# Seven block products in place of eight for the three closing projections of a hybrid encoder step

## The chip, the core and the metric

The kernel runs on one core of one Trainium2 chip. Its time is the device time in microseconds (us) of one execution; several executions are timed and their median is the result. The engines of the core work side by side and are ordered only by semaphores: PE (the matrix engine, with PEld for its weight loads), DVE (vector), ACT (scalar), POOL (GpSimd) and SP, which here does nothing but issue the transfers, in the order of its queue. The profile is one execution taken by the hardware profiler.

## The reference, cut to what matters

One layer of a streaming encoder for 2048 prompt rows and 64 sample rows of width 1024, all in float32. The change lies in the last function alone; `att` and `pb` are the outputs of the two token mixers, `ga`, `gb` and `mg` columns of the input projection.

```python
h = rmsnorm(x, norm_g)
q, k, v, ga, u, gb, mg = split_proj(h, w_in)
att = stick_breaking(q, k_all, v_all)
pb = multi_scale_pool(u, buf, w_pool, pool_scale)

def merge_out(x, att, ga, pb, gb, mg, w_br_a, w_br_b, w_out):
    y_a = (att * jax.nn.silu(ga)) @ w_br_a
    y_b = (pb * jax.nn.silu(gb)) @ w_br_b
    gate = jax.nn.sigmoid(mg)
    m = gate[..., :D_MODEL] * y_a + gate[..., D_MODEL:] * y_b
    return x + m @ w_out

y = rmsnorm(merge_out(...), final_g)
```

The three products with `w_br_a`, `w_br_b` and `w_out` are each 2112 rows by 1024 by 1024.

## The kernel before

A float32 product is made of three matmuls of split operands. `split` (lines 79 and 80) writes `hi`, the operand rounded by a cast on ACT, and `lo`, what is left, by a subtraction on DVE; a product is `hi*hi + hi*lo + lo*hi`, the third small term left out.

The program is in three stretches. The first, up to line 880, makes projections, attention and pooling, a half of the rows at a time. It leaves in DRAM, transposed (channels by rows), the gated attention `aT_d`, the gated pooling `bT_d` and the merge gates `sm_d`. The second (lines 881 to 914) is the last fifteen slabs of the input projection (`proj`, lines 282 to 284), 128 columns each. Beside them `load_weight` brings `w_br_a` into SBUF, split into tiles of 128 rows by 512 columns, and `load_rows` the first block of rows. The raw parts come through a ring of two buffers, `wraw`.

The third stretch is the closing phases, from line 916. It opens tile pools of its own: `back` in SBUF and `bpsum` in PSUM, in the place that the pools of the first stretch gave up. `branch` runs twice, with `aT_d` and `w_br_a`, then with `bT_d` and `w_br_b`. For each block of 424 rows (`POST`) and each 128 output columns it adds 24 matmuls in one PSUM bank (lines 952 to 954: weights stationary, rows moving), multiplies the bank by the gate `sg` on DVE (line 956), adds in the second run the first run's result `mpl` (line 958), and stores the tile `bo` (line 959). The first run's output is `mp_d`, the second's `m_d`. The weights of the next run are loaded and split while this one works.

The output projection (lines 967 to 1027) takes row tiles of 128. There the split rows are stationary and the split `w_out` moves, 512 columns a matmul: two banks of 24 matmuls a tile (lines 1014 to 1016). The residual `xo` is added on DVE (line 1017), ACT sums the squares (line 1019), `rsqrt_of_mean` (lines 82 to 91) makes the scale on DVE and ACT, and line 1025 scales and line 1027 stores. The 64 sample rows take 32 matmuls (lines 1003 and 1006).

PE works in the order written in the program. The order of the other engines and of SP is made by the framework when it compiles: an instruction may be set earlier than it is written if its buffers and inputs are free then, but on the chip each queue is strictly in that fixed order. The framework also sets all semaphores, from the tiles that instructions read and write and from the buffers (`bufs=`) of each pool.

## Time and profile before

| | us |
|---|---|
| median of 3 executions (2823.55 to 2825.31) | 2824.5 |
| span of the profiled execution, first to last instruction | 2823.3 |
| last fifteen slabs of the input projection | 2092 to 2260 |
| both branch projections, first to last matmul start | 2260.4 to 2628.9 |
| output projection, first to last matmul start | 2629.5 to 2815.4 |
| from there to the end | 7.9 |

A row of a group in the profile names line, engine and operation, the tiles (output<-inputs), the shape (partitions x columns), the count, and after the bar the busy time in us and the mean of one in ns. Spans of matmuls overlap, since they are pipelined, so what one matmul costs is read from the distance of two starts, not from its span. In the view of transfers the last number of a row is the median time from issue to landing.

### The profile page before, as it was taken

To read this page: it belongs to the slowest core of one execution; us is meant where nothing else is said; L and a number is where in the kernel's file an instruction comes from. 1 tells how busy PE (TensorE), PEld (TensorE's weight loads), DVE (VectorE), ACT (ScalarE), POOL (GpSimd) and SP (SyncE) were. 2 spreads that over 40 slices of the span, in tenths; PEclk is the share of its full clock that TensorE was granted. 3 is DMA by queue.
4 is the path that set the end of the run, shared out by engine and by line. 5 is a ranking of instruction groups with operands and counts; after the bars stand their busy time and mean duration, and the time that the engine had idled before them with its cause. 6 is when DMAs were issued, how large, how long until landed. Compare 5 with 4: busy or idle time off the path is not lost.

```text
span 2823.3 us, 42058 instructions
## 1 busy us (share of the span) xinstructions
PE 2771.4 (98%) x15044; PEld 2415.1 (86%) x15044; DVE 1678.2 (59%) x2847; ACT 1194.2 (42%) x2500; POOL 447.9 (16%) x1107
## 2 busy tenths in 40 slices
PE   6999999999999999999999999999999999999998
PEld 5988898889998988888888888887778899999877
DVE  6555555577768683578887888885442022434543
ACT  4445444455555553455555555553223111211221
POOL 2112222220000002233343334330000000000000
PEclk9999999999999999999999999999999999999999
DMA  4223222234444454211111111113344264666432
GB/s 148 73 87 125 71 71 71 84 106 157 151 149 149 155 164 127 72 46 49 57 53 46 49 57 53 34 57 98 116 127 148 75 210 142 214 193 199 162 130 88
DMA packets 333309, 307.83 MB, mean 109 GB/s; under 512 B 30302, under 2 KB 288078, under 8 KB 333100
## 3 DMA queue, kind: packets, MB, share of 16 engines
q1 hardware_dynamic: 333100, 305.15, 34.4%
q8 instruction: 118, 1.93, 0.3%
q14 instruction: 91, 0.75, 0.1%
HBM read 208.99 MB, written 96.07 MB: 108 GB/s over the span
## 4 chain that ended last, share of the span: by engine, by line
PE 93%; DVE 4%; ACT 1%; DMA 1%; issue 1%; POOL 0%; SPq 0%; DVEq 0%; ACTq 0%; POOLq 0%
PE pj L282 17%; PE pj L284 17%; PE pj L283 17%; PE ps L952 4%; PE ps L953 4%; PE ps L954 4%; PE tr L636 4%; PE att L653 2%; PE att L652 2%; PE att L651 2%; PE ps L1015 2%; PE z L625 2%; PE ps L1016 2%; PE ps L1014 2%; PE z L624 2%; PE z L623 2%
## 5 line engine op out<-in xcount | busy, mean ns | idle before, releaser
L282 PE MATMUL pj<-hhi,whi 128*128 128x512 f32 (+2 forms) x2608 | 945.2, 362 | 0.0
L284 PE MATMUL pj<-hhi,wlo 128*128 128x512 f32 (+2 forms) x2608 | 917.9, 352 | 0.5 <-DVE wlo L80 0.5
L283 PE MATMUL pj<-hlo,whi 128*128 128x512 f32 (+2 forms) x2608 | 916.8, 352 | 0.1
L284 PEld LDWEIGHTS pj<-hhi,wlo 128*128 128x128 f32 x2608 | 491.9, 189 | 65.9 <-DVE wlo L80 1.0
L282 PEld LDWEIGHTS pj<-hhi,whi 128*128 128x128 f32 x2608 | 494.4, 190 | 59.6 <-ACT sgm L300 0.4
L283 PEld LDWEIGHTS pj<-hlo,whi 128*128 128x128 f32 x2608 | 493.4, 189 | 58.8 <-DVE hlo L80 0.4
L577 DVE TENSOR_TENSOR_SCAN om<-om 128x513 f32<-128x513 f32 (+3 forms) x356 | 388.0, 1090 | 212.5 <-POOL om L559 108.2
L567 ACT ACTIVATE om<-z 128x512 f32<-128x512 f32 (+2 forms) x320 | 171.3, 535 | 323.0 <-PE z L625 273.9
L80 DVE TENSOR_TENSOR wlo<-raw,whi 128x512 fp32r<-128x512 f32 x248 | 171.6, 696 | 199.8 <-ACT whi L79 198.8
L580 DVE TENSOR_TENSOR be<-be,om 128x512 f32<-128x512 f32 (+3 forms) x356 | 230.4, 647 | 31.4
L79 ACT CAST whi<-raw 128x512 fp32r<-128x512 f32 x256 | 158.1, 623 | 171.4 <-PE pj L283 154.0
L79 ACT CAST a<-tr 128x512 fp32r<-128x512 f32 (+2 forms) x356 | 188.1, 528 | 100.4 <-PE tr L636 89.7
L80 DVE TENSOR_TENSOR a<-tr,a 128x512 fp32r<-128x512 f32 (+2 forms) x356 | 215.8, 607 | 23.8 <-ACT a L79 21.7
L952 PE MATMUL ps<-rhi,bwhi 128*128 128x424 f32 (+1 forms) x640 | 226.7, 354 | 0.8 <-issue 0.8
L953 PE MATMUL ps<-rlo,bwhi 128*128 128x424 f32 (+1 forms) x640 | 226.8, 354 | 0.0
L954 PE MATMUL ps<-rhi,bwlo 128*128 128x424 f32 (+1 forms) x640 | 226.3, 354 | 0.0
L579 POOL COPY carry<-om 128x1 f32<-128x1 f32 x356 | 77.9, 219 | 921.7 <-DVE om L577 881.2
L79 ACT CAST rhi<-rraw 128x424 fp32r<-128x424 f32 (+4 forms) x128 | 66.3, 523 | 293.2 <-PE ps L954 221.6
L956 DVE TENSOR_TENSOR bo<-ps,sg 128x424 f32<-128x424 f32 (+1 forms) x80 | 47.8, 597 | 228.7 <-PE ps L954 216.3
L636 PE MATMUL tr<-ident,be 128*128 128x128 f32 x1088 | 176.0, 274 | 6.1 <-DVE be L580 3.6
L636 PEld LDWEIGHTS tr<-ident,be 128*128 128x128 f32 x1088 | 136.5, 140 | 44.9 <-DVE be L580 8.1
L568 ACT ACTIVATE be<-z 128x512 f32<-128x512 f32 (+2 forms) x320 | 170.1, 532 | 0.0
(180 smaller groups left out, 4111.3 us busy)
## 6 DMA issues: line engine op xcount, KB each, us to landing
raw<-in_w_in_dram SPq DMA_DIRECT2D x256, 256.0 KB, 3.1
kraw<-in_cache_k_dram SPq DMA_DIRECT2D x64, 256.0 KB, 3.5
vraw<-in_cache_v_dram SPq DMA_DIRECT2D x64, 256.0 KB, 2.9
sg<-sm_d SPq DMA_DIRECT2D x64, 212.0 KB, 2.6
sm_d<-sgm SPq DMA_DIRECT2D x48, 256.0 KB, 2.1
out_dram<-nat SPq DMA_DIRECT2D x42, 256.0 KB, 2.3
aT_d<-ao SPq DMA_DIRECT2D x32, 256.0 KB, 2.0
xo<-in_x_prompt_dram SPq DMA_DIRECT2D x16, 512.0 KB, 3.6
```

Of the source, the lines that this page charges most:

```text
L79: nc.scalar.copy(hi, src)
L80: (nc.gpsimd if eng == "g" else nc.vector).tensor_tensor(lo, src, hi.bitcast(F32), op=ALU.subtract)
L282: nc.tensor.matmul(ps[:, 0:n], whi[:, k], hhi[:, k, c0:c0 + n], start=k == 0, stop=False)
L283: nc.tensor.matmul(ps[:, 0:n], whi[:, k], hlo[:, k, c0:c0 + n], start=False, stop=False)
L284: nc.tensor.matmul(ps[:, 0:n], wlo[:, k], hhi[:, k, c0:c0 + n], start=False, stop=k == KT - 1)
L567: nc.scalar.activation(om[:, off:512], z[:, off:512], AF.Sigmoid, scale=-SCALE)
L577: nc.vector.tensor_tensor_scan(rev, rev, rev, 1.0, op0=ALU.mult, op1=ALU.bypass)
L580: nc.vector.tensor_tensor(be[:, off:512], be[:, off:512], om[:, off + 1:513], op=ALU.mult)
L636: nc.tensor.transpose(tr[:, i * P:(i + 1) * P], be[:, off + j * P:off + (j + 1) * P], ident)
L952: nc.tensor.matmul(ps[:, 0:n], whi[:, ws], hi[:, 0:n], start=k == 0, stop=False)
L953: nc.tensor.matmul(ps[:, 0:n], whi[:, ws], lo[:, 0:n], start=False, stop=False)
L954: nc.tensor.matmul(ps[:, 0:n], wlo[:, ws], hi[:, 0:n], start=False, stop=k == KT - 1)
```

## The change

Each 1024 by 1024 weight is cut into four blocks of 512 by 512, and the rows into pairs of blocks, so that a projection is a two by two product of blocks. Eight block products are replaced by seven, with sums of blocks as operands: the weight in seven forms (`WFORMS`: three plain blocks, four sums `t1` to `t4`) and the rows in seven forms (`r11`, `r12`, `s2`, `s1`, `r21`, `r12`, `r22`, of which the later `r21` and `r12` hold sums). Accumulators `x` and `y` in PSUM are read out in the midst of their accumulation (`kept`, `okept`), since a part of the sum serves several outputs.

`weight_sums` makes the sums of a weight on POOL and stores them in DRAM (`tw_d`). `load_form` loads and splits one form into a buffer of its own, so that all seven forms of a weight lie in SBUF; the buffer of a form is refilled for the next weight after its last use (`t == 2`). All raw parts of weights pass the ring of two buffers `wraw`, now 512 KB each. In the two branch projections 2112 rows are three pairs of 352 (`NR`). For each branch `i`, pair `t` and form `p` a pass of 48 matmuls runs, `make(s + 2)` preparing the row form two passes on, in two buffers; passes 1, 4, 5 and 6 end outputs (`emit`). The output projection takes pairs of 128-row tiles, 84 matmuls of 512 columns a pair; the sample rows keep plain products, of 40 matmuls, from the forms that are there. The rest of `out_sample`, `residual` and `finish` hold the same steps as before.

```diff
@@ constants and DRAM @@
-NB = 424
-POST = ((0, 424), (424, 424), (848, 424), (1272, 424), (1696, 416))
+NR = 352
+WFORMS = ("b11", "b21", "t2", "t1", "t3", "b22", "t4")
+    tw_d = dram.tile([3, 4, D // 2, D // 2], F32, name="tw_d")
@@ beside the last fifteen slabs of the input projection @@
-        wside = ctx.enter_context(tc.tile_pool(name="wside", bufs=1, side="right"))
-        def load_weight(w, out):
...
-        def load_rows(src, r0, n, into, out):
...
+        wright = ctx.enter_context(tc.tile_pool(name="wright", bufs=1, side="right"))
+        rowx = ExitStack()
+        rform = rowx.enter_context(tc.tile_pool(name="rform", bufs=1, side="right"))
+        wpool = {nm: wright for nm in WFORMS[:4]}
+        weights = (w_br_a[0], w_br_b[0], w_out[0])
+        def weight_sums(i):
+            for k in range(4):
+                top, bot = (wright.tile([P, 2, 512], F32, name="wraw", bufs=2) for _ in range(2))
+                for h, t in enumerate((top, bot)):
+                    r = h * 512 + k * P
+                    nc.sync.dma_start(t, weights[i][r:r + P, :].rearrange("p (j c) -> p j c", j=2))
+                b11, b12, b21, b22 = top[:, 0], top[:, 1], bot[:, 0], bot[:, 1]
+                for j, out, x, y in ((0, b11, b12, b11), (2, b12, b22, b12), (1, b22, b22, b11), (3, b21, b21, b22)):
+                    nc.gpsimd.tensor_tensor(out, x, y, op=ALU.subtract)
+                    nc.sync.dma_start(tw_d[i, j, k * P:(k + 1) * P, :], out)
+        def load_form(i, nm):
+            if nm[0] == "t":
+                src = tw_d[i, int(nm[1]) - 1]
+            else:
+                r, c = (int(x) - 1 for x in nm[1:])
+                src = weights[i][r * 512:(r + 1) * 512, c * 512:(c + 1) * 512]
+            sv = src.rearrange("(k p) c -> p k c", p=P)
+            hi = wpool[nm].tile([P, 4, 512], F32R, name=f"{nm}hi")
+            lo = wpool[nm].tile([P, 4, 512], F32R, name=f"{nm}lo")
+            for k in (0, 2):
+                raw = wright.tile([P, 2, 512], F32, name="wraw", bufs=2)
+                nc.sync.dma_start(raw, sv[:, k:k + 2])
+                split(hi[:, k:k + 2], lo[:, k:k + 2], raw)
+            return hi, lo
+        def row_form():
+            return (rform.tile([P, 4, NR], F32R, name="rhi", bufs=2),
+                    rform.tile([P, 4, NR], F32R, name="rlo", bufs=2))
+        wf, rf = {}, {}
+        def before_closing():
+            yield from weight_sums(0)
+            for nm in WFORMS[:4]:
+                wf[0, nm] = load_form(0, nm)
+                yield 1.0
+            for p in range(2):
+                hi, lo = rf[p] = row_form()
+                for k in (0, 2):
+                    raw = wright.tile([P, 2, 512], F32, name="wraw", bufs=2)
+                    src = aT_d[p * 512 + k * P:p * 512 + (k + 2) * P, 0:NR].rearrange("(k p) r -> p k r", p=P)
+                    nc.sync.dma_start(raw[:, :, 0:NR], src)
+                    split(hi[:, k:k + 2], lo[:, k:k + 2], raw[:, :, 0:NR])
+                yield 1.0
+        run((chain(*[proj(GROUPS_B, [merge_gate(1, c)]) for c in range(1, 2 * KT)]), 15 * slab_ns(1)),
+            (before_closing(), 11.0))
@@ the two branch projections @@
-        def branch(w, src, gate0, dst, add, rows0=None):
...
-        branch(wa, aT_d, 0, mp_d, None, rows0)
-        rows0 = rows_of(bT_d, *POST[0])
-        wb = weight(w_br_b[0])
-        branch(wb, bT_d, D, m_d, mp_d, rows0)
+    wleft = ctx.enter_context(tc.tile_pool(name="wleft", bufs=1, side="left"))
+    wpool.update((nm, wleft) for nm in WFORMS[4:])
+    def product(ps, stat, mov, first, cols, rows):
+        for k in range(4):
+            nc.tensor.matmul(ps, stat[0][:, k, cols], mov[0][:, k, rows], start=first and k == 0, stop=False,
+                             skip_group_check=True)
+            nc.tensor.matmul(ps, stat[0][:, k, cols], mov[1][:, k, rows], start=False, stop=False,
+                             skip_group_check=True)
+            nc.tensor.matmul(ps, stat[1][:, k, cols], mov[0][:, k, rows], start=False, stop=k == 3,
+                             skip_group_check=True)
+    with rowx:
+        rowp = rowx.enter_context(tc.tile_pool(name="rowp", bufs=1, side="left"))
+        psum = rowx.enter_context(tc.tile_pool(name="bpsum", bufs=2, space=PSUM))
+        order = [(i, t, p) for i in range(2) for t in range(3) for p in range(7)]
+        raws = {}
+        def load_rows(i, t):
+            src = (aT_d, bT_d)[i]
+            for nm in ("r11", "r12", "r21", "r22"):
+                a, b = int(nm[1]) - 1, int(nm[2]) - 1
+                raws[nm] = rowp.tile([P, 4, NR], F32, name=nm)
+                r0 = (2 * t + a) * NR
+                nc.sync.dma_start(raws[nm], src[b * 512:(b + 1) * 512, r0:r0 + NR].rearrange("(k p) r -> p k r", p=P))
+        def sums():
+            raws["s1"] = rowp.tile([P, 4, NR], F32, name="s1")
+            raws["s2"] = rowp.tile([P, 4, NR], F32, name="s2")
+            nc.gpsimd.tensor_tensor(raws["s1"], raws["r21"], raws["r22"], op=ALU.add)
+            nc.vector.tensor_tensor(raws["s2"], raws["s1"], raws["r11"], op=ALU.subtract)
+            nc.gpsimd.tensor_tensor(raws["r21"], raws["r11"], raws["r21"], op=ALU.subtract)
+            nc.vector.tensor_tensor(raws["r12"], raws["r12"], raws["s2"], op=ALU.subtract)
+        def make(s):
+            if s >= len(order):
+                return
+            i, t, p = order[s]
+            if p == 0:
+                load_rows(i, t)
+            if s > 1:
+                rf[s] = row_form()
+                split(rf[s][0], rf[s][1], raws[("r11", "r12", "s2", "s1", "r21", "r12", "r22")[p]])
+            if p == 1:
+                sums()
+        x1, x2, x5, xs_, ys_ = {}, {}, {}, {}, {}
+        def kept(ps, name):
+            t = rform.tile([P, 2, NR], F32, name=name, tag="kept", bufs=4)
+            nc.scalar.copy(t, ps)
+            return t
+        def emit(i, t, a, c, src, other):
+            cs = slice(c * P, (c + 2) * P)
+            rs = slice((2 * t + a) * NR, (2 * t + a + 1) * NR)
+            sg = rowp.tile([P, 2, NR], F32, name="sg", bufs=4)
+            nc.sync.dma_start(sg, sm_d[i * D + c * P:i * D + (c + 2) * P, rs].rearrange("(j p) r -> p j r", p=P))
+            if i:
+                mp = rowp.tile([P, 2, NR], F32, name="mp", bufs=2)
+                nc.sync.dma_start(mp, mp_d[cs, rs].rearrange("(j p) r -> p j r", p=P))
+            if other is not None:
+                nc.vector.tensor_tensor(other, src, other, op=ALU.add)
+                src = other
+            nc.vector.tensor_tensor(sg, src, sg, op=ALU.mult)
+            if i:
+                nc.vector.tensor_tensor(sg, sg, mp, op=ALU.add)
+            nc.sync.dma_start((mp_d, m_d)[i][cs, rs].rearrange("(j p) r -> p j r", p=P), sg)
+        later = chain(weight_sums(1), weight_sums(2))
+        make(0)
+        for nm in WFORMS[4:]:
+            wf[0, nm] = load_form(0, nm)
+        make(1)
+        for s, (i, t, p) in enumerate(order):
+            r = rf.pop(s)
+            for cc in range(2):
+                if p == 0:
+                    xs_[cc] = psum.tile([P, 2, 512], F32, name="x")
+                elif p in (1, 3):
+                    ys_[cc] = psum.tile([P, 2, 512], F32, name="y")
+                acc = (xs_ if p in (0, 2, 4, 6) else ys_)[cc]
+                for j in range(2):
+                    c = 2 * cc + j
+                    product(acc[:, j, 0:NR], wf[i, WFORMS[p]], r, p in (0, 1, 3),
+                            slice(c * P, (c + 1) * P), slice(0, NR))
+                out = acc[:, :, 0:NR]
+                if p == 0:
+                    x1[cc] = kept(out, "x1")
+                elif p == 1:
+                    emit(i, t, 0, 2 * cc, out, x1[cc])
+                elif p == 2:
+                    x2[cc] = kept(out, "x2")
+                elif p == 3:
+                    x5[cc] = kept(out, "x5")
+                elif p == 4:
+                    emit(i, t, 1, 4 + 2 * cc, out, x5[cc])
+                elif p == 5:
+                    emit(i, t, 0, 4 + 2 * cc, out, x2[cc])
+                else:
+                    emit(i, t, 1, 2 * cc, out, None)
+            make(s + 2)
+            if 2 <= s < 14:
+                next(later, None)
+            if t == 2:
+                wf[i + 1, WFORMS[p]] = load_form(i + 1, WFORMS[p])
@@ the output projection @@
     with ExitStack() as back:
         pool = back.enter_context(tc.tile_pool(name="back", bufs=1, side="left"))
-        psum = back.enter_context(tc.tile_pool(name="bpsum", bufs=8, space=PSUM))
...
+        fpool = back.enter_context(tc.tile_pool(name="bform", bufs=1, side="right"))
+        psum = back.enter_context(tc.tile_pool(name="opsum", bufs=2, space=PSUM))
...
+        def rows_of(r0, n):
+            t = [pool.tile([P, 4, 256], F32, name=nm, bufs=2) for nm in ("mt", "mb")]
+            for h in range(2):
+                nc.sync.dma_start(t[h][:, :, 0:n], m_d[h * 512:(h + 1) * 512, r0:r0 + n].rearrange("(k p) r -> p k r", p=P))
+            return t
...
+        def out_forms(r0):
+            top, bot = rows_of(r0, 256)
+            r11, r21, r12, r22 = top[:, :, 0:P], top[:, :, P:], bot[:, :, 0:P], bot[:, :, P:]
+            out = {}
+            def put(names, srcs):
+                hi = fpool.tile([P, len(names), 4, P], F32R, name=f"{names[0]}hi")
+                lo = fpool.tile([P, len(names), 4, P], F32R, name=f"{names[0]}lo")
+                for j, (nm, src) in enumerate(zip(names, srcs)):
+                    split(hi[:, j], lo[:, j], src)
+                    out[nm] = (hi[:, j], lo[:, j])
+            put(("a11", "a12"), (r11, r12))
+            s12 = pool.tile([P, 4, P], F32, name="s1o")
+            s2 = pool.tile([P, 4, P], F32, name="s2o")
+            nc.gpsimd.tensor_tensor(s12, r21, r22, op=ALU.add)
+            nc.vector.tensor_tensor(s2, s12, r11, op=ALU.subtract)
+            put(("s2", "s1"), (s2, s12))
+            nc.gpsimd.tensor_tensor(r21, r11, r21, op=ALU.subtract)
+            nc.vector.tensor_tensor(r12, r12, s2, op=ALU.subtract)
+            put(("s3", "s4"), (r21, r12))
+            put(("a22",), (r22,))
+            return out
+        def okept(ps, name, add=None, m=P):
+            t = pool.tile([P, 512], F32, name=name, tag="okept", bufs=3)
+            nc.scalar.copy(t[0:m], ps)
+            return t
+        def add3(xt, bs, ps, other):
+            if other is not None:
+                nc.gpsimd.tensor_tensor(xt[:, bs], xt[:, bs], other, op=ALU.add)
+            nc.vector.tensor_tensor(xt[:, bs], ps, xt[:, bs], op=ALU.add)
+        left, right = slice(0, 512), slice(512, 1024)
+        whole = slice(0, 512)
+        def out_pair(f, xts):
+            cols = slice(0, P)
+            x = psum.tile([P, 512], F32, name="ox")
+            product(x, f["a11"], wo["b11"], True, cols, whole)
+            x1 = okept(x, "x1")
+            z = psum.tile([P, 512], F32, name="oy")
+            product(z, f["a12"], wo["b21"], True, cols, whole)
+            add3(xts[0], left, z, x1)
+            product(x, f["s2"], wo["t2"], False, cols, whole)
+            x2 = okept(x, "x2")
+            y = psum.tile([P, 512], F32, name="oy")
+            product(y, f["s1"], wo["t1"], True, cols, whole)
+            x5 = okept(y, "x5")
+            product(x, f["s3"], wo["t3"], False, cols, whole)
+            add3(xts[1], right, x, x5)
+            product(y, f["s4"], wo["b22"], False, cols, whole)
+            add3(xts[0], right, y, x2)
+            product(x, f["a22"], wo["t4"], False, cols, whole)
+            add3(xts[1], left, x, None)
+        def out_sample():
+            top, bot = rows_of(1024, DEC)
+            both = [fpool.tile([P, 2, 4, P], F32R, name=nm) for nm in ("a11hi", "a11lo")]
+            for h, src in enumerate((top, bot)):
+                t = both[h]
+                split(t[:, 0, :, 0:DEC], t[:, 0, :, DEC:P], src[:, :, 0:DEC])
...
+        pairs = [(half * RA + i * P, half * 1024 + i * P) for half in range(2) for i in range(0, 8, 2)]
+        ahead = out_forms(pairs[0][0])
+        for n, (r0, r) in enumerate(pairs):
+            f = ahead
+            xts = [residual(xp[r + i * P:r + (i + 1) * P], P) for i in range(2)]
+            out_pair(f, xts)
+            if n + 1 < len(pairs):
+                if n == 5:
+                    out_sample()
+                ahead = out_forms(pairs[n + 1][0])
+            for i in range(2):
+                finish(xts[i], P, yp[r + i * P:r + (i + 1) * P])
```

## What is predicted

> **What bounds the kernel now.** The page comes first, then the lines of the two closing stages, then single rows of the timeline.
>
> ```profile
> span 2823.3 us, 42058 instructions
> PE 2771.4 (98%) x15044; PEld 2415.1 (86%) x15044; DVE 1678.2 (59%) x2847; ACT 1194.2 (42%) x2500; POOL 447.9 (16%) x1107
> PE 93%; DVE 4%; ACT 1%; DMA 1%; issue 1%; POOL 0%; SPq 0%; DVEq 0%; ACTq 0%; POOLq 0%
> 2450.00:2629.00 179.00, 179.00 (x933) 174.74 (x932) 75.66 (x130) 28.27 (x51) 0.00 (x0) 1.00 0.63 199
> 2629.00:2816.00 187.00, 186.74 (x804) 149.56 (x802) 85.41 (x224) 47.30 (x126) 5.28 (x16) 1.00 0.37 121
> ```
>
> The chain that ended last is 93% PE, and in the second branch and the output projection (the two windows: length, then busy PE, PEld, DVE, ACT, POOL, clock, DMA share, GB/s) PE has no gap, with DVE under half busy. So a matmul less is time less, until something else is late. The price of a matmul is the distance of starts:
>
> ```profile
> L952 PE MATMUL ps<-rhi,bwhi x640: 344/356/428, 2260.4 to 2628.9; 128*128 128x424 f32 x128, 128*128 128x416 f32 x32
> L1014 PE MATMUL ps<-bwhi,rhi x256: 387/394/398, 2629.5 to 2814.9; 128*128 128x512 f32 x128
> 2815.35 0.39 PE L1016 MATMUL ps<-bwlo,rhi 128*128 128x512 f32 x1
> 60.86 0.31 PE L284 MATMUL pj<-hhi,wlo 128*128 128x320 f32 x1
> ...
> 63.94 0.31 PE L284 MATMUL pj<-hhi,wlo 128*128 128x320 f32 x1
> 2300.03 0.19 PEld L954 LDWEIGHTS ps<-rhi,bwlo 128*128 128x128 f32 x1
> ```
>
> - Branches: 3 lines of 640 make 1920 matmuls in 2629.5 - 2260.4 = 369.1 us, 192.2 ns each for 422.4 columns on average.
> - Output: 768 matmuls and the sample's 32, from 2629.5 to the start of the last, 2815.35: 185.85 / 799 = 232.6 ns.
> - 320 columns: 21 distances in 3.08 us, 146.7 ns. A weight load lasts 190 ns, yet the matmuls follow at 146.7, so the load doesn't set the distance here.
>
> For the new 352 columns I interpolate between 320 and 422.4: 146.7 + 32 x 45.5 / 102.4 = 160.9 ns (bounds 160 to 161.3, by the price of a column at 512 and at 320).
>
> The Trainium skill, "TensorE: Matmul & The Clock Gate", section "Back-to-back issue gap", gives N / 2.4 + 2.5 ns warm: 149.2 ns for 352, an estimate by which the branches would gain 24 us more (2770 in all). The same formula gives 178.5 for 422.4 columns where this trace has 192.2, so the rows decide and it gets no chance of its own.
>
> **The change part by part.** *PE.* The branches have 2 x 3 x 7 passes of 48 = 2016 matmuls at 160.9 = 324.4 us: 44.7 less. A pass is 7.72 us, a block of seven 54.1. The output has 8 x 84 + 40 = 712 matmuls instead of 800: 88 x 0.2326 = 20.5 less. Together **-65.2 us**. Everything below gives some of it back.
>
> *First border.* The new pools lie where the old ones lay. How such a border was passed before:
>
> ```profile
> 2259.69 0.60 ACT L300 ACTIVATE sgm<-pj 128x512 f32<-128x512 f32 x1 [4.98 <-PE pj L284]
> 2260.36 0.19 PEld L952 LDWEIGHTS ps<-rhi,bwhi 128*128 128x128 f32 x1 [1.19 <-issue]
> SPq L944 <- DMA sm_d<-sgm: 1.6, 1, 1.6
> 2262.59 1.74 SPq L944 DMA_DIRECT2D sg<-sm_d  x4
> SPq L892 <- DMA bT_d<-gbl: 1.6, 1, 1.6
> 2270.00:2280.00 10.00, 10.00 (x54) 9.72 (x53) 5.86 (x11) 3.77 (x7) 0.00 (x0) 1.00 0.97 321
> 2100.00:2260.00 160.00, 159.60 (x686) 128.51 (x684) 31.79 (x48) 42.37 (x77) 0.00 (x0) 1.00 0.37 118
> xo<-in_x_prompt_dram SPq DMA_DIRECT2D x16, 512.0 KB, 3.6
> m_d<-bo SPq DMA_DIRECT2D x32, 212.0 KB, 2.5
> sm_d<-sgm SPq DMA_DIRECT2D x48, 256.0 KB, 2.1
> ```
>
> The first closing matmul started when ACT had read the last old bank (2260.29), though the new pool has eight banks and seven were free; the first gate load waited for the last store out of the old pool (2262.59), and the first load of `w_br_a`, a border earlier, likewise for a store of `gbl`. I read it so: nothing enters a new pool until all in the old one is done with.
>
> The first two passes and their weights have forms made beforehand: the slabs' 160 us, with POOL idle and DVE and ACT at 32 and 42 us, hold four sums of 10.5 and twelve raw parts of some 3 (both below), 78 in all. The third pass needs `s2`, that is the four row blocks, 2.88 MB, in the new pool. Counted from PE's end of the slabs (2259.6): issue from 3.0, 9.0 us at 321 GB/s and 2 us to land: 14. Then, by the rows below, POOL's sum of 1408 columns (3.6 to 5.1), DVE (1.6), ACT (1.4), DVE (1.6), four signals: ready at 23.3 or so. PE asks at 0.8 + 2 x 7.72 = 16.3. **+7** (3 if the loads needn't wait, 11 if the weight parts come between).
>
> ```profile
> L657 POOL TENSOR_TENSOR ao<-ao,sga 128x512 f32<-128x512 f32 x32 | 42.4, 1325 | 54.2 <-ACT ao L656 48.4 <-DMA raw<-in_w_in_dram 5.6
> L80 POOL TENSOR_TENSOR klo<-kback,khi 128x512 fp32r<-128x512 f32 x16 | 29.7, 1862 | 12.8 <-ACT khi L79 12.8
> L80 DVE TENSOR_TENSOR bwlo<-wraw,bwhi 128x512 fp32r<-128x512 f32 x32 | 20.6, 689 | 8.8 <-ACT bwhi L79 8.8
> L80 DVE TENSOR_TENSOR rlo<-rraw,rhi 128x256 fp32r<-128x256 f32 x8 | 3.3, 424 | 1.5 <-ACT rhi L79 1.5
> L79 ACT CAST bwhi<-wraw 128x512 fp32r<-128x512 f32 x32 | 19.0, 622 | 50.9 <-PE ps L953 37.3 <-DMA wraw<-in_w_br_b_dram 6.8 <-DMA wraw<-in_w_out_dram 6.5
> L79 ACT CAST rhi<-rraw 128x256 fp32r<-128x256 f32 x8 | 3.2, 402 | 6.2 <-PE ps L1016 4.7 <-DMA rraw<-m_d 1.4
> L88 DVE TENSOR_TENSOR acc<-rs 128x1 f32<-128x1 f32 x16 | 2.6, 163 | 0.5
> 34.28 0.69 PE L457 MATMUL tr<-ident,kst 128*128 128x128 f32 x2 [5.56 <-DVE hlo L80]
> 34.28:38.00 3.72, 3.72 (x18) 3.72 (x19) 3.62 (x11) 0.75 (x2) 0.97 (x1) 0.50 0.14 39
> 38.00:41.00 3.00, 2.44 (x18) 2.23 (x16) 3.00 (x3) 1.18 (x2) 2.46 (x2) 0.88 0.00 1
> ```
>
> Columns beyond the first 512 cost DVE 1.035 ns and ACT 0.86: 704, 1024 and 1408 columns take DVE 0.89, 1.22, 1.62 and ACT 0.79, 1.06, 1.39.
>
> *Clock.* After 5.56 us without work PE had half its clock for 3.72 us and a good 0.7 more: some 4.4 us, half of them lost. A stop of 7 us or more should cost that again: **+2.2** at each border.
>
> The Trainium skill speaks against the change here: the same page, "Part 1: The HAM clock gate", says that an idle window of about 3.4 us halves the clock. The trace agrees (0.50 after 5.56 us).
>
> *Passes.* A block asks of DVE seven splits (11.3), two sums (3.2) and fourteen to twenty-two reads of 704 (12.5 to 19.6), and fourteen weight splits in the third block (17.1): 27 to 34 us of 54.1, and 44 to 51 in a third block. ACT has at most 29.4, POOL 7.3 for rows. Each form has a pass to be made in (3.0 us of 7.72), each bank half a pass to be read. So nothing must wait but where DVE is nearly full, at the end of branch two, and where SP holds a load behind a store that waits. Between 0 (PE idled 0.4 us of 160 in the slabs) and 15 (a landing of 2.5 us at each of six blocks) I take **+6**, near the lower row.
>
> The sums of the second and third weight stand ahead of `w_br_b`'s forms in the ring of two raw buffers. The three late forms of `w_br_a` pass it first, from 3.0 on, each 4.0 to load, 1.06 on ACT and two times 1.22 on DVE: free at 3 + 3 x 7.5 = 25. A sum step is three subtractions (3 x 1.33), a store (0.4 + 2.1) and a load (0.4 + 3.6): 10.5 us with a free queue. I take 14, since the first branch moves, in 171 us, rows 11.5, gates 8.7, results 8.7, late forms 3.1, sums 8.4 in and 8.4 out and the next forms 7.3, 56 MB or 327 GB/s, more than the 321 of the fullest row. Eight steps end at 137. The second branch starts at 0.8 + 9.2 + 21 x 7.72 = 172, and its first form needs some 10 us: in time while a step is under 17. No term of its own.
>
> *Second border.* The row forms, the banks and the buffers from which `m_d` is stored give way to the output's. After the last pass: DVE 1.8, store 0.5 + 2.5, three loads of 512 KB (0.9 to issue, 3.6 to 6 to land), ACT 0.62, DVE 0.69, signals: 11 to 13 us where there were 0.4. **+11.5** (2 if space is handed on by address: then only `lo` of the first form waits for the last pass) **+2.2** for the clock.
>
> *Output.* A pair asks of DVE seven splits, two sums and four reads of 512 columns (13 x 0.69), and for two tiles seven short operations (0.16) and the scaling (1.41): 14.0 of 84 x 0.2326 = 19.5 us. Stops of 0 to 1 us a pair: **+3**. The sample uses the buffers of `a11`, so the pair behind it waits for a cast and a subtraction: **+1.6**.
>
> *End.*
>
> ```profile
> 2815.78 0.69 DVE L1017 TENSOR_TENSOR xo<-ps,xo 128x512 f32<-128x512 f32 x1 [4.90 <-PE ps L1016]
> 2816.56 0.63 ACT L1019 ACTIVATE bjk<-xo 128x512 f32<-128x512 f32 x1 [4.88 <-DVE xo L1017]
> 2818.90 1.41 DVE L1025 SCALAR_TENSOR_TENSOR xo<-xo,rs,fg_bc 128x512 f32<-128x512 f32 x2
> ```
>
> Both squares of the last tile now follow its last add, and another tile's scaling (1.41) stands beside: **+1.5**.
>
> Sum: 7 + 2.2 + 6 + 11.5 + 2.2 + 3 + 1.6 + 1.5 = 35.0 back of 65.2: span 2823.3 - 30.2 = 2793.1. The median lies 1.2 above the profiled span: **2794**.
>
> **The rivals.**
> - *Borders passed by address.* The first costs 4, the second 2, and both stay under the 5.56 us that cooled the clock: 3 + 9.5 + 4.4 = 17 less, **2777**. For it: new tiles need only their own bytes. Against: three waits above.
> - *Late forms.* Steps of 20 us end at 185, `w_br_b`'s first form is ready at 195, 23 late, of which the 6 above hold some 3: **2814**. For it: the queue is full there. Against: the ring slows itself, and what else is loaded then is wanted a pass or more later.
> - *The ring becomes the bound: slower.* From steps of 21 us the lateness, 31, eats the 30 gained; at 25 the first form comes at 235, 63 late: **2854**. It takes two landings a step some 5 to 7 us longer than the 2.1 and 3.6 quoted.
> - *The change doesn't do what it says*: if 352 columns cost what 422 do, held by the 190 ns of a weight load, 2016 x 192.2 = 387.5, 18.4 more: **2857**. Against it stand 146.7 ns at 320 with the same load.
>
> **How the numbers follow.** Forecast 0.55, by address 0.20, late forms 0.11, slower by the ring 0.08, no cheaper matmuls 0.02, and 0.04 for sums of these near the old time. A measurement can tell about 0.2%, 5.6 us. So faster 0.86, same 0.04, slower 0.10. The range is 2770, below the second case, to 2816, above the third; it leaves out 0.06 below and 0.14 above.
>
> **What would show it.** Distances of 161 ns at 352 columns; a stop of PE near 2276 with a halved clock behind it; a second stop of over 10 us ahead of the first 512-column matmul, ended by the load of `m_d`, ACT and DVE; PE at 54 to 55 us a block between. Wrong it is if the second stop is short, if PE waits at the first pass of the second branch for `w_br_b`'s forms, or if each pass waits on DVE.

## The result and the profile after

| | before | after | predicted |
|---|---|---|---|
| median (us) | 2824.9 (4 runs) | 2857.2 (4 runs, 2855.8 to 2859.6) | 2794, range 2770 to 2816 |
| ratio to before, 95% interval | | 1.0116 [1.0101, 1.0130] | 0.989 |
| span of the profiled execution | 2823.3 | 2854.0 | 2793.1 |

The change makes the kernel 32 us slower. It was forecast to be 30 us faster, so the sign is wrong too. First the head of the page of the changed kernel, then three views of its trace: two rows of PE's timeline, the windows of the closing stages (columns as in the prediction: length, busy time and count of PE, PEld, DVE, ACT, POOL, then clock, DMA share, GB/s), and PE's groups, whose last column is the idle time ahead of the group and what ended it.

```profile
span 2854.0 us, 41869 instructions
PE 2721.7 (95%) x15052; PEld 2375.8 (83%) x15052; DVE 1818.1 (64%) x2831; ACT 1269.9 (44%) x2528; POOL 621.5 (22%) x1191
PE 81%; DVE 6%; DMA 6%; POOL 2%; issue 2%; ACT 2%; SPq 0%; DVEq 0%; POOLq 0%; ACTq 0%
```

```profile
2439.77 0.32 PE L953 MATMUL x<-rlo,t2hi 128*128 128x352 f32 x1
...
2445.96 0.32 PE L953 MATMUL x<-rlo,t2hi 128*128 128x352 f32 x1
```

```profile
2421.40:2477.00 55.60, 55.60 (x335) 55.60 (x336) 41.82 (x34) 24.16 (x24) 9.63 (x3) 0.95 0.86 278
2352.20:2357.00 4.80, 4.80 (x16) 4.80 (x17) 0.89 (x1) 0.00 (x0) 2.71 (x3) 0.50 0.66 238
2674.20:2679.20 5.00, 5.00 (x12) 3.91 (x13) 3.37 (x4) 3.00 (x5) 3.07 (x2) 0.50 1.07 378
```

```profile
L951 PE MATMUL x<-rhi,b11hi 128*128 128x352 f32 x96 | 35.8, 373 | 47.4 <-DVE sg L1014 46.6 <-issue 0.8
L951 PE MATMUL x<-rhi,t2hi 128*128 128x352 f32 x96 | 31.7, 330 | 3.3 <-ACT rhi L81 3.3
L953 PE MATMUL x<-rlo,t2hi 128*128 128x352 f32 x96 | 31.7, 330 | 6.5 <-DVE rlo L82 6.5
L951 PE MATMUL ox<-b11hi,a11hi 128*128 128x512 f32 x4 | 2.7, 671 | 15.6 <-ACT a11hi L81 15.6
```

What the reader is to see. The matmuls became as cheap as forecast: 39 distances of starts in 6.19 us, 158.7 ns each at 352 columns (160.9 forecast). The third block takes 55.6 us once it has begun, with all the splits of the next weight in it: DVE works 41.8 of them and PE never waits. PE is 50 us less busy than before. But the chain that ended last is only 81% PE, where it was 93%, and PE's idle time stands in a few places. The first product of a block waits 46.6 us in all for `sg` of L1014, DVE's gate multiply; the third pass waits 9.8 at the first border (3.3 and 6.5 in the rows), the output 15.6 at the second. Behind the stops of 19.0 and 15.6 us the clock is 0.50 for about 5 us, and behind one of 6.8 it is the same (behind those of 6.0 and 6.5 the mean of 5 us is 0.72 and 0.61):

```profile
2601.90:2607.00 5.10, 5.10 (x17) 5.10 (x18) 5.10 (x5) 0.00 (x0) 0.00 (x0) 0.50 0.99 321
```

How the 95.9 us come about that the profiled run lies above 2823.3 - 65.2 = 2758.1:

| | predicted | in the trace |
|---|---|---|
| price of a matmul, 2016 x (158.7 - 160.9) | 0 | -4.4 |
| slabs: a cast ahead of a gate on ACT | 0 | +5.3 |
| first border, third pass | +7 | +9.8 |
| starts of the six blocks ("passes") | +6 | +46.6 |
| second border | +11.5 | +15.6 |
| output and sample | +4.6 | +3.5 |
| end, from the last matmul's start | +1.5 | +0.8 |
| clock | +4.4 | +18.7, as what is left |

Eight stops were over 3 us; 18.7 / 8 = 2.3 us each is about the price that the prediction gave to one (2.2), and half of the 4.8 us at 0.50 above. So of the 61 us that were missed, 40.6 are block starts and some 14 the clock behind stops that weren't foreseen.

**Why a block starts late.** The first product of a block needs the bank `x` that the last pass of the block before has filled, and DVE frees it by L1014. Here is the longest case, PE's stop of 19.0 us at 2333, in the timelines of PE, DVE, POOL and SP (start, length, what, idle time before it and what ended it).

```profile
2352.19 0.63 PE L951 MATMUL x<-rhi,b11hi 128*128 128x352 f32 x1 [18.98 <-DVE sg L1014]
```

```profile
2342.53 1.63 DVE L978 TENSOR_TENSOR s<-s,r 128x1408 f32<-128x1408 f32 x1 [13.56 <-POOL s L977]
2344.07 4.57 DVE L82 TENSOR_TENSOR rlo<-r,rhi 128x1408 fp32r<-128x1408 f32 x1
2348.67 2.57 DVE L980 TENSOR_TENSOR r<-r,s 128x1408 f32<-128x1408 f32 x1
2351.16 0.88 DVE L1014 TENSOR_TENSOR sg<-x,sg 128x704 f32<-128x704 f32 x1
```

```profile
2332.64 5.29 POOL L900 TENSOR_TENSOR wraw<-wraw 128x512 f32<-128x512 f32 x4 [7.15 <-DMA wraw<-in_w_br_b_dram]
2339.35 3.15 POOL L977 TENSOR_TENSOR s<-r,r 128x1408 f32<-128x1408 f32 x1 [1.42 <-DMA r<-aT_d]
2342.57 4.59 POOL L979 TENSOR_TENSOR r<-r,r 128x1408 f32<-128x1408 f32 x1
```

```profile
2328.57 0.44 SPq L1017 DMA_DIRECT2D mp_d<-sg  x1
2333.93 0.33 SPq L901 DMA_DIRECT2D tw_d<-wraw  x1
2334.31 0.43 SPq L971 DMA_DIRECT2D r<-aT_d  x1
```

Read from below. SP issues nothing from 2329.0 to 2333.9: the next thing in its queue is a store of the weight sums, whose subtraction POOL makes only at 2332.64. Behind that store stands the load of a row block (2334.31). POOL needs the block for L977 (2339.35), DVE needs that sum for L978 (2342.53), and DVE's queue holds L978, a split and L980 ahead of the multiply that PE waits for. The bank that the multiply reads was full by 2333.2, when PE stopped. POOL is busy for most of the stop, but it isn't its time that is short: it had been free for 1.42 us when the row block landed. PE, DVE, POOL and SP stand idle one for another.

The second long stop (12.4 us) has the same root on a shorter way: between 2380 and 2425 SP waits for POOL's subtractions of the ring again, and the gate load of the multiply itself is behind them (SP's waits: us in all, times, longest; then DVE's and SP's rows).

```profile
SPq L901 <- POOL wraw L900: 13.8, 9, 2.6
```

```profile
2420.34 0.89 DVE L1014 TENSOR_TENSOR sg<-x,sg 128x704 f32<-128x704 f32 x1 [13.65 <-DMA sg<-sm_d]
```

```profile
2413.00 0.84 SPq L1007 DMA_DIRECT2D sg<-sm_d  x1
```

PE had stopped at 2409.0. So some 4 us of this stop are the late issue of the load, and 7.3 its landing, which is long beside the 4.1 us of the page's median for these loads: what SP had held back went out at once, ten transfers between 2409.2 and 2415.9.

In the second branch there are no weight sums. The stops are 6.0 and 6.8, and DVE's row stands out in another way:

```profile
2531.11 1.63 DVE L978 TENSOR_TENSOR s<-s,r 128x1408 f32<-128x1408 f32 x1 [4.04 <-POOL s L977]
2532.65 3.87 DVE L1014 TENSOR_TENSOR sg<-x,sg 128x704 f32<-128x704 f32 x1
```

```profile
2531.15 4.62 POOL L979 TENSOR_TENSOR r<-r,r 128x1408 f32<-128x1408 f32 x1
```

DVE waits for POOL's sum, and then a multiply with both inputs in the buffers (here `x` is a kept copy and no bank), which takes 0.88 us elsewhere, takes 3.87; it ends at 2536.5, when POOL's two-input subtraction has ended (2535.8). The multiply that PE waits for comes behind it.

### The profile page after: what moved, and what is told of

Read it like the earlier page. It is cut to its first block, busy times and chain, and to the rows that moved or that the text cites. A ratio compares the mean times of both kernels' runs of the same rounds, so it can differ in the third digit from the quotient of the medians.

```text
span 2854.0 us, 41869 instructions
## 1 busy us (share of the span) xinstructions
PE 2721.7 (95%) x15052; PEld 2375.8 (83%) x15052; DVE 1818.1 (64%) x2831; ACT 1269.9 (44%) x2528; POOL 621.5 (22%) x1191
## 4 chain that ended last, share of the span: by engine, by line
PE 81%; DVE 6%; DMA 6%; POOL 2%; issue 2%; ACT 2%; SPq 0%; DVEq 0%; POOLq 0%; ACTq 0%
PE pj L284 16%; PE pj L285 16%; PE pj L286 16%; PE tr L638 4%; PE att L655 2%; PE att L654 2%; PE att L653 2%; PE z L627 2%; PE z L626 2%; PE z L625 2%; POOL wraw L900 1%; PE x L951 1%; PE x L953 1%; PE x L955 1%; PE y L951 1%
## 5 line engine op out<-in xcount | busy, mean ns | idle before, releaser
L653 PE MATMUL att<-a,v 128*128 128x512 f32 (+1 forms) x320 | 133.5, 417 | 0.0
L900 POOL TENSOR_TENSOR wraw<-wraw 128x512 f32<-128x512 f32 x48 | 72.7, 1515 | 254.7 <-DMA sm_d<-sgm 173.3
L561 POOL TENSOR_SCALAR_AFFINE_SELECT om<-om 128x128 f32<-128x128 f32 x128 | 50.8, 397 | 354.2 <-ACT om L569 354.1
L574 POOL COPY om<-carry 128x1 f32<-128x1 f32 x224 | 123.9, 553 | 2.7 <-DVE be L582 0.7
L655 PE MATMUL att<-a,v 128*128 128x512 f32 (+1 forms) x320 | 118.6, 371 | 3.6 <-DVE a L82 3.3
```

What stands on the lines that cost most here:

```text
L653: nc.tensor.matmul(self.acc[:, s], vhi[:, js], ahi[:, s], start=first, stop=False)
L655: nc.tensor.matmul(self.acc[:, s], vhi[:, js], alo[:, s], start=False, stop=last)
```

## The experiments

Theory Q: time is lost because each engine takes its queue strictly in a fixed order that puts things that wait ahead of things that are urgent, on SP above all and on DVE. Rivals: D, the added transfers fill the DMA engines; P, POOL has not the time for the weight sums; C, POOL and DVE hold each other up. All kernels were timed beside the kernel before (medians of 2824.5 to 2824.9). "Block starts" is PE's idle time ahead of the first product of blocks two to six, as in the group row above.

| run | median us | ratio, 95% interval | block starts us | second border us |
|---|---|---|---|---|
| the change | 2857.2 | 1.0116 [1.0101, 1.0130] | 46.6 | 15.6 |
| no weight sums | 2834.8 | 1.0036 [1.0023, 1.0049] | 26.5 | 15.2 |
| order | 2844.0 | 1.0073 [1.0058, 1.0088] | 37.4 | 16.3 |
| both | 2812.2 | 0.9957 [0.9943, 0.9972] | 5.9 | 16.5 |
| order, stores by POOL | 2853.5 | 1.0104 [1.0081, 1.0127] | 37.6 | 15.3 |
| late stores | 2839.2 | 1.0054 [1.0039, 1.0069] | 33.6 | 15.6 |
| late stores, order | 2827.0 | 1.0008 [0.9998, 1.0018] | 25.0 | 17.0 |
| the same, rows first | 2815.0 | 0.9962 [0.9949, 0.9975] | 17.1 | 15.7 |
| late stores, order, sums on DVE | 2815.4 | 0.9969 [0.9958, 0.9981] | 8.5 | 15.1 |
| these four and a pause | 2809.7 | 0.9950 [0.9933, 0.9966] | 16.2 | 15.1 |
| the same, early rows | 2803.0 | 0.9921 [0.9906, 0.9936] | 15.8 | 5.1 |
| the same, slow ring | 2793.2 | 0.9887 [0.9870, 0.9903] | 11.1 | 5.5 |
| the same, three `mp` | 2791.7 | 0.9884 [0.9869, 0.9899] | 8.1 | 5.5 |

### No weight sums, DVE's order, and both

```
-        later = chain(weight_sums(1), weight_sums(2))
+        later = iter(())
...
-                src = tw_d[i, int(nm[1]) - 1]
+                j = int(nm[1]) - 1
+                src = tw_d[0, j] if i == 0 else weights[i][j // 2 * 512:(j // 2 + 1) * 512, j % 2 * 512:(j % 2 + 1) * 512]
```

The sums of the second and third weight are left out, so these two weights' products are not the layer's.

> Leaves out the sums of the second and third weight inside the branch loop; the forms t1 to t4 of these weights are loaded from plain blocks of the weight instead (same loads, other values). Theory Q (fixed queue order): the stops of PE at the start of the second and third block (19.0 and 12.4 us in the profile of the changed kernel) come from SP, which stands at the stores of the weight sums and waits for POOL while row and gate loads are queued behind them, so they fall to 7 us or less, like the later ones (2 to 7 us), and the later ones stay; with the clock that they cost some 25 to 30 us go: about 2829 us. Rival D (the transfer queue is full): the bytes fall by 17 MB in the first branch alone, so the two stops go too, but the stops of the second branch, where nothing was taken away, stay. Rival P (POOL and DVE hold each other up): as Q, and DVE operations of 1408 columns fall from 2.3 to 2.7 us back to 1.6 in the first branch.

```
+            if p == 6:
+                with tc.issue_after(mult.ins):
+                    make(s + 2)
+            else:
+                make(s + 2)
-            make(s + 2)
```

Here `mult` is the multiply of L1014 that the last pass of a block emits; what DVE makes for the next block is queued behind it.

> All work kept; on DVE the sums and the split of the next block's second form are queued behind the gate multiplications of a block's last pass. Theory Q: these multiplications free the banks that the next block's first pass writes, and on DVE they stand behind sums that wait for POOL and for a row load; so the stops of 2.0, 6.1 and 6.8 us at the later block starts go, and of the 19.0 the part that was DVE's order, some 10; the 12.4, where the multiplication waited for its gate load, stays. Some 25 to 30 us with the clock: about 2830 us. Rival D: the bytes are the same, so all stops stay: 2857. Rival P: POOL's row sums and the multiplications collide less, the later stops shrink to 1 to 3 us.

> Both edits, with the sums of the second and third weight left out. Theory Q: no stop over 1 us at any block start; left are the two borders (9.8 and 15.6 us), the 5 us in the slabs and small ones in the output: 2857 - 47 of stops - 12 of clock = about 2798 us. Rival D: the second branch still stops 6 us at a block, about 2815.

Each alone shortens the block starts (46.6 to 26.5 and to 37.4), and both together leave 5.9; the time falls by 22, 13 and 45 us. The two act in series: a load freed on SP doesn't help while DVE's queue holds the multiply behind the next block's sums, and the multiply gains little by going first while its own gate is held on SP. With both the kernel is faster than before. All three were slower than theory Q said (2829, 2830 and 2798). Without the sums the two long stops fell to 4.7 and 5.3 us, as expected, but the start of the second branch grew from 2.0 to 4.9. With the order the three later starts (2.0, 6.0 and 6.8) didn't go but became 5.0, 3.5 and 3.4. With both, one start of 3.4 us stayed, and the slabs' stop and the second border were longer than in the change (5.8 for 4.3, 16.5 for 15.6). What this leaves open is which part of the weight sums hurts: without them their bytes, POOL's work and SP's queue all go at once. The sign that rival P named came too: between 2295 and 2480, 8 of 23 DVE operations of 1408 columns took over 2 us in the change, and 1 of 28 without the sums.

### Stores of the sums from POOL's queue

```
-                    nc.sync.dma_start(tw_d[i, j, k * P:(k + 1) * P, :], out)
+                    nc.gpsimd.dma_start(tw_d[i, j, k * P:(k + 1) * P, :], out)
```

> All work kept: the order of e2, and the stores of the weight sums issued from POOL's own queue in place of SP's. Theory Q: SP no longer waits for POOL, the row and gate loads go out in time, and no stop over 2 us is left at a block start: 2800 to 2808 us, near e3, and the 5 us in the slabs go too, where SP stood at the same stores. Rival D: same bytes as the changed kernel, so the stops of 19.0 and 12.4 us stay at least in half: 2830 or more. If POOL pays for issuing, a sum step grows by some 1 us a store, and the second weight's forms may come late.

A miss: 2853.5, slower than the order alone. The block starts are the same in sum (37.6 for 37.4), in other places: 4.6 us for 11.8 at the second block, 24.0 for 13.8 at the third. The rest is lost in the slabs, where the stop that was to go grew from 5.5 to 10.2 us and the first closing matmul starts 8.6 us later. SP's waits between 2385 and 2432, and DVE's multiply behind them:

```profile
SPq L897 <- DMA tw_d<-wraw: 25.5, 5, 6.9
```

```profile
2428.28 0.89 DVE L1014 TENSOR_TENSOR sg<-x,sg 128x704 f32<-128x704 f32 x1 [26.88 <-DMA sg<-sm_d]
```

SP no longer waits at the stores, but at the next thing of the same ring, the load into a buffer whose store has yet to land. Nothing was won by moving one half of a ring that still turns as fast as it can. By the reading that the next runs test, what blocks SP is that a step of some 15 us is asked for in every pass of 7.7.

### Late stores, without and with the order

```
                     nc.gpsimd.tensor_tensor(out, x, y, op=ALU.subtract)
+                yield 1.0
+                for j, out in ((0, b11), (2, b12), (1, b22), (3, b21)):
                     nc.sync.dma_start(tw_d[i, j, k * P:(k + 1) * P, :], out)
                 yield 1.0
...
-            if 2 <= s < 14:
+            if 2 <= s < 14 or 22 <= s < 28:
```

The stores of the first weight's sums, beside the slabs, move in the same way.

> All the work is kept; a step of the weight sums issues its four stores one pass later than its subtractions, and the second set of sums is spread over two branches, so that SP no longer comes to a store before POOL has made it. Theory Q (fixed queues: SP stands at the ring's stores, DVE's order puts the next block's sums ahead of the multiply that frees a bank): the second stop (12.4 us) falls under 5, the first (19.0) to some 5 to 10 because r22 is loaded in time but DVE's order stays; with the clock behind them 2832 to 2840. Rival D (the transfers of the ring fill the DMA engines, whoever waits): the same bytes move, the time stays within 6 us of 2857. Rival P (POOL's time for the ring is what is short): the same, 2850 or more.

> The late stores, and DVE's row sums queued behind the multiplies of the last pass. All the work is kept. Theory Q: both places at which a queue stood are gone, so the block starts look like those of the run without sums and with the order (0 to 3.5 us each); 2812 to 2822, under the kernel before. Rival D or P: 2835 to 2845, as with the order alone (2844).

Here the sums are made, with the same bytes and the same work for POOL in all, only later. The time falls by 18 us without the order and by 17 beyond the order alone (2844.0 to 2827.0), so neither total sets the time. The rate hardly fell either: a step is asked for every 15.4 us, where in the change the steps came 14.4 us apart, and between 2300 and 2400 POOL works 52.8 us in the change and 51.1 with late stores and the order, and the DMA engines move 248 and 265 GB/s. Here are the windows of the longest stop of the change, and of a stretch of the run "early rows" below in which PE works 43 of 47 us:

```profile
2333.00:2353.00 20.00, 1.02 (x5) 0.84 (x4) 9.48 (x4) 1.36 (x1) 18.11 (x9) 0.62 0.69 225
```

```profile
2353.00:2400.00 47.00, 42.97 (x253) 42.71 (x252) 26.69 (x22) 11.54 (x11) 13.41 (x8) 0.93 0.90 304
```

The transfers weren't at their limit where PE stood longest (0.69 and 225 GB/s for 0.90 and 304). So D and P in their plain form, "it is the bytes" and "it is POOL's time", don't hold. But the two long stops of theory Q didn't go as it said either: one stop of 13 to 16 us stayed in each run, ahead of the third block, where under 5 was expected; in the run without the order one of 10.3 us came in the second branch, where two steps of the ring now run; and the second kernel missed its range by 5 us. With the order, SP still comes to its stores before POOL's subtractions are done (2.9 us of waiting between 2384 and 2400); the stores of the gated products go out behind them, and the next gate loads wait 5.4 us for those to land before their buffers are free; the multiply's row has 16.18 us of waiting for its load. A step every other pass is hardly slower than the ring itself.

### Rows first, and the row sums on DVE

```
-            for nm in ("r11", "r12", "r21", "r22"):
+            for nm in ("r21", "r22", "r11", "r12"):
...
         make(0)
-        for nm in WFORMS[4:]:
-            wf[0, nm] = load_form(0, nm)
         make(1)
...
+            if s < 3:
+                wf[0, WFORMS[4 + s]] = load_form(0, WFORMS[4 + s])
```

> As the run before, and behind the first border the rows are loaded ahead of the three late weight forms, r21 and r22 first. Theory: the stop in the third pass (6.5 us) and the 3.3 us ahead of it are the order of the loads on SP behind the border; they go to under 2 us together, 7 to 10 us less than the run before with the clock. Rival: the wait is the border's own (old pools come free too late for three passes); the stops move to the late forms' passes and less than 3 us is won.

The stops at the first border's third pass go from 10.2 to 4.2 (under 2 was expected), and the time by 12 us, of which the rest is shorter block starts (25.0 to 17.1), which also have their rows loaded in the new order. POOL's first sum starts 6.8 us after the issue of the rows, where it took 10.6 in the change. So the stop was in good part the order of the loads, and with it of the weight splits that follow them on DVE.

```
-            nc.gpsimd.tensor_tensor(raws["s1"], raws["r21"], raws["r22"], op=ALU.add)
+            nc.vector.tensor_tensor(raws["s1"], raws["r21"], raws["r22"], op=ALU.add)
...
-            nc.gpsimd.tensor_tensor(raws["r21"], raws["r11"], raws["r21"], op=ALU.subtract)
+            nc.vector.tensor_tensor(raws["r21"], raws["r11"], raws["r21"], op=ALU.subtract)
```

> As the late stores with the order, and the two row sums that POOL makes are made on DVE. Rival C (POOL's two-input operations hold DVE's up, 0.89 us to 3.87): the multiplies and splits beside them are back at 0.9 and 1.6 us, and the block starts in the second branch lose 2 to 3 us each, 3 to 8 us in all. Against it: DVE gets 2 x 1.6 us more a block, which was POOL's 7.8; if DVE's own time is what ends the block starts, 3 to 8 us slower.

11.6 us faster than late stores with the order, though DVE has 3.2 us more to do a block. DVE's groups, first with the sums on POOL, then on DVE:

```profile
L82 DVE TENSOR_TENSOR rlo<-r,rhi 128x1408 fp32r<-128x1408 f32 x28 | 58.2, 2080 | 47.6 <-ACT rhi L81 47.6
L1014 DVE TENSOR_TENSOR x<-y,x 128x704 f32<-128x704 f32 x24 | 21.3, 887 | 12.7 <-PE y L957 12.3
L980 DVE TENSOR_TENSOR s<-s,r 128x1408 f32<-128x1408 f32 x6 | 12.3, 2057 | 3.9 <-POOL s L979 3.9
```

```profile
L82 DVE TENSOR_TENSOR rlo<-r,rhi 128x1408 fp32r<-128x1408 f32 x28 | 48.1, 1720 | 46.7 <-ACT rhi L81 46.7
L1014 DVE TENSOR_TENSOR x<-y,x 128x704 f32<-128x704 f32 x24 | 21.3, 887 | 13.9 <-PE y L957 13.7
L980 DVE TENSOR_TENSOR s<-s,r 128x1408 f32<-128x1408 f32 x6 | 9.7, 1620 | 0.0
```

The same splits of 1408 columns take 1.72 us in place of 2.08, L980 1.62 in place of 2.06. The addition whose one input is a bank (`x<-y,x`) takes 0.887 in both, and four of them that ran beside POOL in the change took 0.88 or 0.89 each. So C is real for operations that read both inputs from the buffers, and not for those that read one from a bank. The Trainium skill, "GPSIMD Engine Reference", section "Key points", says this: the two engines share their ways to the buffers, and an instruction of VectorE with two inputs from there contends. The section gives no size; here a split took a fifth longer on average, and one multiply four times as long. The run doesn't part this from the other thing that it removes, DVE's waits for POOL's sum (4.04 us in the row of the change above); how much of the 11.6 us each has is open.

### These four and a pause, then the second border

```
             yield from weight_sums(0)
+            yield 1.0
             for nm in WFORMS[:4]:
```

> All the work is kept: late stores, DVE's order, row sums on DVE, rows first behind the first border, and one pause more between the weight sums and the first form in the slabs, so that ACT's cast of that form is not queued ahead of the slab's while its load waits for the ring. Theory Q with C: the stops add up, 2815.4 less some 7 for the border's order and 3 to 6 for the slabs, with the clock behind them: 2802 to 2808. Rival: one limit stands behind all of them (DVE's or the transfers' time), a stop that goes comes back at the next block; then no less than 2812.

2809.7, a little above the expected 2802 to 2808 and below the rival's 2812. The first border is nearly gone (0.8 in the third pass), but the block starts are back from 8.5 to 16.2 with the other order of the loads: a part of what goes in one place does come back at the next. And no effect of the pause is seen: PE's stop in the slabs was 4.5 us here and 2.7 to 3.4 in the three later runs with it, 4.3 in the change and 2.8 to 6.4 in the other runs that store from SP. Its cause is seen in the change on ACT and SP:

```profile
2143.77 1.04 ACT L81 CAST b11hi<-wraw 128x1024 fp32r<-128x1024 f32 x1 [12.74 <-DMA wraw<-in_w_br_a_dram]
...
2145.24 0.59 ACT L302 ACTIVATE sgm<-pj 128x512 f32<-128x512 f32 x1
```

```profile
2135.07 3.06 SPq L901 DMA_DIRECT2D tw_d<-wraw  x3
...
2138.70 0.53 SPq L916 DMA_DIRECT2D wraw<-in_w_br_a_dram  x1
```

ACT's cast of the first form waits 12.7 us for a load that stood behind the ring's stores, and the slab's gate, which frees PE's bank, is queued behind that cast. The pause in the program's text didn't move the cast in ACT's queue: here too it stands ahead of the gate and waits 13.4 us. A stop of 2.7 us or more stayed in all versions.

```
+    rowr = ctx.enter_context(tc.tile_pool(name="rowr", bufs=1, side="left"))
...
+            if s == 40:
+                early = rows_of(0, 256)
...
-            t = [pool.tile([P, 4, 256], F32, name=nm, bufs=2) for nm in ("mt", "mb")]
+        t = [rowr.tile([P, 4, NR], F32, name=nm) for nm in (("r11", "r12"), ("r21", "r22"))[turn[0] % 2]]
```

> As the run before, and the pool of r11 to s2 stays open into the output, whose first rows of m are loaded into r11, r12 while the last blocks run; the gain vector and the sums of the output's rows take s2 and s1. Theory of the second border: its 15 us are pool release, landing of the stores to m and the new loads one behind the other, though the rows wanted first were stored 150 us earlier; with these loads ahead only the release of the form buffers and one cast stay, 15 goes to 2 to 5 us and the clock's loss behind it with it: 10 to 14 us less than the run before. Rival: the stop is the last weight form and the DVE queue behind it, and less than 4 us is won.

In the change, the second border ran like this on DVE, SP and ACT:

```profile
2660.37 1.82 DVE L1016 TENSOR_TENSOR sg<-sg,mp 128x704 f32<-128x704 f32 x2 [0.97 <-DMA mp<-mp_d]
```

```profile
2662.23 0.36 SPq L1017 DMA_DIRECT2D m_d<-sg  x1
2666.78 0.35 SPq L1065 DMA_DIRECT2D fg_bc<-in_final_g_dram  x1
2667.18 0.43 SPq L1071 DMA_DIRECT2D mt<-m_d  x1
```

```profile
2673.44 0.62 ACT L81 CAST a11hi<-mt 128x512 fp32r<-128x512 f32 x1 [7.56 <-DMA mb<-m_d]
```

Even the gain vector, which depends on nothing, is loaded only when the last store from the old pool has landed, 4.5 us after its issue; another 6.3 pass from `mt`'s issue to the cast. With the pool kept open, PE's first output product:

```profile
2616.38 0.76 PE L954 MATMUL ox<-b11hi,a11hi 128*128 128x512 f32 x1 [5.12 <-DVE sg L1027]
```

15.1 us became 5.1, ended by the last gate multiply. The border was the pool's release and what came one by one behind it. The medians fell by 6.8 us and the spans of the two profiled runs by 9.4 (2808.0 to 2798.6), against 10 to 14 expected: the place is right, the gain a little smaller.

### A slow ring, three buffers

```
                 yield 1.0
+                yield 1.0
                 for j, out in ((0, b11), (2, b12), (1, b22), (3, b21)):
...
-            if 2 <= s < 14 or 22 <= s < 28:
+            if 2 <= s < 14 or 22 <= s < 34:
```

> As the run with the early rows, and a step of the weight sums takes three passes in place of two, with the stores two passes behind the subtractions. In the run before, SP stood 5.3 us at a store for POOL ahead of the multiply's load at the first block start (6.5 us of stop). Theory Q: the stops at the first two block starts (6.5 and 4.0) go to under 2 us, the later ones (1.4, 3.9) stay: with the clock 2787 to 2796. Rival D (what is left is transfers that are late because the queue of them is full): the ring's bytes are the same, under 4 us is won.

```
-                mp = rowp.tile([P, 2, NR], F32, name="mp", bufs=2)
+                mp = rowp.tile([P, 2, NR], F32, name="mp", bufs=3)
```

> As the run before, with three buffers for the first branch's part (mp) in place of two. In the second branch DVE stood 4.4 and 2.9 us for a load of mp that could only be issued once the add two before it had freed its buffer. Theory: the stop of 3.9 us in the second branch goes and the one at the output (5.1) gets shorter: 3 to 7 us less than the run before. Rival: SP's order holds the load, not the buffer; within 2 us of the run before.

SP's and DVE's rows of the run before, and PE's group of the slow ring:

```profile
2313.44 5.29 SPq L903 DMA_DIRECT2D tw_d<-wraw  x4
2318.77 0.98 SPq L1020 DMA_DIRECT2D sg<-sm_d  x2
```

```profile
2323.98 1.79 DVE L1027 TENSOR_TENSOR sg<-x,sg 128x704 f32<-128x704 f32 x2 [9.51 <-DMA sg<-sm_d]
```

```profile
L955 PE MATMUL x<-rhi,b11hi 128*128 128x352 f32 x80 | 27.3, 341 | 11.1 <-DVE sg L1028 11.1
```

With a step in three passes the first two block starts fell from 6.5 and 4.0 us to 3.0 and none, and the time by 9.8 us to 2793.2, at the same bytes: theory Q once more. One start in the second branch grew (3.9 to 7.4), so the sum fell less. The third buffer brought 1.5 us, inside the two intervals; the stop at the output stayed at 5.5. That is the rival's outcome in time, though not quite its mechanism. Between 2440 and 2620 DVE's waits for `mp` fell from 14.1 to 6.1 us, so the buffer had held loads, and the start that had grown went back from 7.4 to 3.6. But SP's waits at the gate loads, for the stores that free their buffers, grew from 30.9 to 44.9 us, and three stops of 1.5 to 1.9 us came elsewhere.

The last version does all the work of the change and is 1.2% faster than the kernel before (0.9884 [0.9869, 0.9899]), 65 us faster than the change as it was written.

## Why the prediction was wrong

- **The price of a matmul: right.** 158.7 ns where 160.9 was interpolated; the rival "no cheaper matmuls" fell. That its time, 2857, is the measured one is chance.
- **The step that failed is "Passes":** "Each form has a pass to be made in (3.0 us of 7.72), each bank half a pass to be read. So nothing must wait but where DVE is nearly full, at the end of branch two, and where SP holds a load behind a store that waits", and the +6 taken for it, "near the lower row". The trace has 46.6. The busy times of that paragraph hold: in the undisturbed third block DVE worked 41.8 of 55.6 us (44 forecast). What was not counted is order. The added up work fits into a pass only if each engine finds the right thing at the head of its queue. SP's and DVE's heads were stores and sums that waited for POOL, whose own head waited for SP. The paragraph names the mechanism, a load behind a store that waits, but gave it one landing of 2.5 us a block; the two worst cases cost 19.0 and 12.4. The Trainium skill, "TensorE: Matmul & The Clock Gate", section "Architectural detail", has ScalarE and VectorE take their queues strictly first in, first out. The traces agree: ACT's gate stood 12.7 us behind a cast, DVE's multiply behind L978.
- **The ring of the weight sums: right in its time, wrong in its term.** The steps were forecast at 14 us; the first began at 2301 and the eighth at 2402, 14.4 apart.

```profile
2301.43 1.29 POOL L900 TENSOR_TENSOR wraw<-wraw 128x512 f32<-128x512 f32 x1 [13.48 <-DMA wraw<-in_w_br_b_dram]
...
2402.01 7.20 POOL L900 TENSOR_TENSOR wraw<-wraw 128x512 f32<-128x512 f32 x4 [7.81 <-DMA wraw<-in_w_out_dram]
```

  The forms of `w_br_b` were in time, as forecast: the product that starts the second branch waits 2.0 us, for DVE's multiply and for no form:

```profile
2479.46 0.40 PE L951 MATMUL x<-rhi,b11hi 128*128 128x352 f32 x1 [2.03 <-DVE sg L1014]
```

  "No term of its own" was wrong all the same: the ring's lateness cost nothing, but its stores and loads stood in SP's queue ahead of rows and gates of the first branch. The slower rival (2854) lies within 3 us of the result only by chance: its mechanism, late forms, isn't in the trace.
- **First border: right in kind, 9.8 for 7, but by another sum.** `s2` came a little sooner than forecast: SP issued all four blocks at once, ahead of the two parts of `b22`, and `s2` is made 18.3 us after PE's end of the slabs (2266.6), where 14 to land and 5.2 to 6.7 for the two sums were taken. What was left out is again a queue: on DVE both splits of `b22`, the first stretched to 4.20 us beside POOL's subtraction, and the sum of L980 stand between `s2` and its split.

```profile
2269.43 2.27 SPq L971 DMA_DIRECT2D r<-aT_d  x4
```

```profile
2284.84 4.20 DVE L82 TENSOR_TENSOR b22lo<-wraw,b22hi 128x1024 fp32r<-128x1024 f32 x1
...
2291.63 1.61 DVE L82 TENSOR_TENSOR rlo<-s,rhi 128x1408 fp32r<-128x1408 f32 x1
```

  With the rows first, the weight parts later and the sums on DVE the third pass is down to 0.8 us.
- **Second border: right in kind, 15.6 for 11.5.** Nothing enters the new pool before the old one's last store has landed; the run with the pool kept open shows it. Mis-sized were DVE's end (3.8 us from the last matmul to the last store's issue, 1.8 taken) and the landing of that store (4.5 us to the next pool's first load, 3.0 taken for issue and landing); the new loads were not (6.3 us, 4.5 to 6.9 taken). The 0.4 us that the prediction had before the change is a misreading: there the last branch matmul starts at 2629.28 (2628.9 is the last of the first of three lines) and the first output matmul at 2629.47, with no stop. The rival "by address" fell.
- **The clock: right for one stop**, and 18.7 us in place of 4.4, because there were eight stops and not two.
- **The slabs weren't foreseen**: 5.3 us there, where the text let POOL, DVE and ACT's free time pay for the forms and did not ask what stands behind the cast that waits.
- **Output, sample, end:** 4.3 for 6.1.

With the queues in better order and the border's loads ahead, the saving on matmuls comes through: the profiled run of the last version lies 34.4 us above 2758.1, and 26.8 of them are stops of PE. That its 2791.7 is close to the 2794 forecast is chance, since the stops are others than those that were added up.

## What to carry to other kernels

Adding up busy time tells whether work can be hidden; whether it will be is decided by what stands at the head of each queue, so for each step that is added write down what it waits for and which urgent instruction of the same queue comes behind it. A background ring (load, compute, store) that shares a queue with urgent loads must be asked for clearly more slowly than it can turn, with each store issued well after its computation: here a turn took 14.4 us, and steps asked for every 23 us (three passes) won back what those every 7.7 and 15.4 lost. And where a stage ends and its buffers are released, the first loads of the next stage belong into buffers that are already free.

## What was not expected of the hardware

- DVE operations with both inputs in the buffers were stretched while POOL ran a two-input operation: 0.88 to 3.87 us for one multiply of 704 columns, 1.62 to 4.57 for one split of 1408. Those with one input in a bank were not (0.887 on average, 0.88 or 0.89 for the four beside POOL). It reads as one operation waiting for the whole of the other: the multiply of 3.87 us ends 0.75 us after POOL's subtraction (its own length is 0.88), the split of 4.57 ends 1.5 us after (its own is 1.62), and POOL's subtraction L979, which starts together with DVE's L978 of 1.63 us, takes 4.59 to 4.62 in both cases, where POOL's sum L977 with DVE idle takes 3.15.
- A store of 256 KB landed 2.2 us after its issue from SP's queue and 3.8 us after its issue from POOL's, in the medians of the pages of the change and of the run with the stores moved.
